# Asking for the up weights of the first pair of hidden tiles earlier in a macaron block

## The chip, the cores and the metric

The kernel runs on one core of one Trainium2 chip, in one launch. The metric is the device time of an execution in microseconds, as the median of several. Lower is better.

The core's engines work side by side, each through its own list of instructions: TensorE (PE in the profile; its weight loads are PEld), VectorE (DVE), ScalarE (ACT), GpSimd (POOL) and SyncE (SP), which issues most of the loads from DRAM. They wait for one another through semaphores.

## The reference

A macaron transformer block for 512 tokens of width 1024, in float32: a gated feed-forward network at half weight, a token mixer (differential and dilated attention), a second feed-forward network, and a last normalisation. The change lies in the two feed-forward networks, whose hidden width is 2816.

```python
def swiglu(x, w_gate, w_up, w_down):
    return (jax.nn.silu(x @ w_gate) * (x @ w_up)) @ w_down

x = x + 0.5 * swiglu(rmsnorm(x, ffn1_norm[layer]), ...)
x = x + token_mixer(rmsnorm(x, mix_norm[layer]), ...)
x = x + 0.5 * swiglu(rmsnorm(x, ffn2_norm[layer]), ...)
return rmsnorm(x, final_norm)
```

## The kernel before

**Layout and precision.** The activations lie transposed: eight tiles x[k] of 128 features by 512 tokens. Every factor of a product is split into a high part, rounded to fp32r, and a low part, the remainder; a product of two such factors is three matmuls (`mm3`, lines 108 to 111: high by high, high by low, low by high).

**A weight tile.** `get_w` (line 103) asks SyncE for 128 x 1024 values into a raw buffer (line 96; three buffers go round, `raw`), gives the tile a place in `w_all` (three places of 1024 high and 1024 low columns go round, `w_place`), rounds it on ACT (line 100) and makes the remainder on DVE (line 101). So a weight tile needs its raw buffer (until DVE has made the remainder of the tile three before it), its place (until PE has done with the tile three before it), the transfer, the cast and the remainder before PE can begin.

**A feed-forward network** (`ffn`, lines 184 to 512, called for "a", the first, and "b", the second) has JF = 22 hidden tiles of 128 and three stages:

- *Raw tiles*, j up to n1 - 1, where n1 (PAIRED) is 6 in "a" and 4 in "b": gate and up products side by side into banks pg and pu, each tile with two weight tiles of four features each (`wgu`, line 475), 48 matmuls of 512 columns. Below n0 (EARLY, 5 and 3) they use features that aren't yet normalised; the last, j = n0, uses the normalised ones, xh and xl. From j = n0 on the order of SyncE and POOL is that of the program text, PE's is so throughout, and on DVE and ACT a scheduler orders the raw tiles.
- *Pairs*, the tiles from n1 on, two by two, with a fast scheme for 2 x 2 blocks of a product: seven products of half size in place of eight, made of sums of weight blocks and of features. A unit is one pair and one side (gate or up). For the first pair only the gate side is such a unit; its up products are plain: `up(n1)` and `up(n1 + 1)` (line 272), 24 matmuls of 512 columns each, in banks of their own.
- *Down products*, eight output tiles of 66 matmuls each.

**Around the first pair.** `units[0]` is the gate side of the first pair, `units[1]` that of the second. What they need is made ahead:

- `weight_sums(j, c)` (line 261) makes two sums of weight blocks in two slots: SyncE loads one block (line 268) and POOL then adds another with an accumulating transfer (line 269). In the trace they are s10 and s30 for the gate side, s11 and s31 for the up side. Those of `units[0]` are asked for in the last raw tile, after k = 0 (line 488), those of `units[1]` as the pairs begin (line 429). In "a" the latter lie in slots 8 and 9, where the normalised features nx 0 and 1 lie until `normed_t(0)` has used them; in "b" they lie in slots 6 and 7.
- `normed_x(p)` makes the normalised features nx and splits them into xh and xl. `normed_t(p)` (line 235) makes their sums and splits them, into the tiles tx and tt of the trace (lines 241 to 257); it is called for p = 0 and 1 in the last raw tile, for p = 2 in `up(n1)` and for p = 3 in `up(n1 + 1)`.
- `load(0)` (line 296) asks for the two raw weight tiles of `units[0]`, raw_s0, in `up(n1)` after k = 2.
- In `up(n1 + 1)` `prepare_step` (line 415) begins to make the operands of the first products of `units[0]`: sums (`total`), casts (`high`, line 323) and remainders (`low`, line 327). They take their places from `w_all` too.

Within the pairs (line 492) DVE and ACT follow the program text as well. The up weights of the first pair, raw_su in the trace, are asked for and split at the start of each up product:

```python
            wh, wl = get_w(wst[j - n1][1], f"su{nm}{j}")
```

The first product of `units[0]` accumulates in a bank pw. With the trace's names the order on PE is: raw tiles on pg and pu, then `up(n1)` and `up(n1 + 1)` on pu, then pw, pz, px and so on.

Of the kernel before, what the change touches and what calls it, by code (L numbers as in the profile page):

```python
# [50 lines left out]
def tile_macaron(ctx: ExitStack, tc, xs, xT, wf, wgu1, wst1, wd1, wqk, wv, wo, wgu2, wst2, wd2,  # L51
# [13 lines left out]
    def slot(i, nm, dt=F32):  # L65
        return sl.tile([P, S], dt, tag=f"slot{i}", name=nm)

    def mm_bank(nm):
        return pp.tile([P, S], F32, tag="mm", name=nm, bufs=4)
# [24 lines left out]
    def load_w(src, nm, n=1024, shift=0):  # L94
        raw = wp.tile([P, 1024], F32, tag="raw", name=f"raw_{nm}")
        nc.sync.dma_start(raw[:, :n], src)
        return (raw, *w_place(shift))

    def split_w(raw, h, l, a, b):
        A.copy(h[:, a:b], raw[:, a:b])  # L100
        V.tensor_tensor(l[:, a:b], raw[:, a:b], h[:, a:b].bitcast(F32), op=ALU.subtract)  # L101

    def get_w(src, nm, n=1024, shift=0):
        raw, h, l = load_w(src, nm, n, shift)
        split_w(raw, h, l, 0, n)
        return h, l

    def mm3(po, wh, wl, mh, ml, first, last, on=False):
        T.matmul(po, wh, mh, start=first, stop=False, skip_group_check=on)  # L109
        T.matmul(po, wh, ml, start=False, stop=False, skip_group_check=on)  # L110
        T.matmul(po, wl, mh, start=False, stop=last, skip_group_check=on)  # L111
# [72 lines left out]
    def ffn(wgu, wst, wd, n0, n1, norm, early, res, nm, hooks, first=None, last_halves=None):  # L184
# [12 lines left out]
        def activated(j, t):  # L197
            h = ah[j] = slot(j, f"ah{nm}{j}", F32R)
            l = al[j] = slot(JF + j, f"al{nm}{j}", F32R)
            A.copy(h[:], t[:])  # L200
            V.tensor_tensor(l[:], t[:], h[:].bitcast(F32), op=ALU.subtract)

        def gate(j, pg, pu):
            t1 = tp.tile([P, S], F32, tag="ptb", name=f"t1{nm}{j}")
            if j < n0:
                bc = res["bc"]
                V.tensor_tensor(t1[:], pg[:], bc[:], op=ALU.mult)
                A.activation(t1[:], t1[:], AF.Silu)
                t2 = tp.tile([P, S], F32, tag="ob", name=f"t2{nm}{j}")
                V.tensor_tensor(t2[:], pu[:], bc[:], op=ALU.mult)  # L210
                V.tensor_tensor(t1[:], t2[:], t1[:], op=ALU.mult)
            else:
                A.activation(t1[:], pg[:], AF.Silu)
                V.tensor_tensor(t1[:], pu[:], t1[:], op=ALU.mult)
            activated(j, t1)
# [45 lines left out]
        def weight_sums(j, c):  # L261

            (a11, _), (a21, a22) = [[wst[j + i - n1][c][:, h * 512:(h + 1) * 512] for h in range(2)]
                                    for i in range(2)]
            sums[j, c] = []
            for i, (a, b) in enumerate(((a21, a22), (a11, a21))):
                t = slot(c * JF + j + i, f"s{2 * i + 1}{c}{nm}{j}")
                nc.sync.dma_start(t[:], a)
                nc.gpsimd.dma_start(t[:], b, accum_op=ALU.add)
                sums[j, c].append(t)  # L270

        def up(j):

            wh, wl = get_w(wst[j - n1][1], f"su{nm}{j}")
            pu = ups[j] = pp.tile([P, S], F32, tag="t", name=f"pu{nm}{j}", bufs=2)
            for k in range(KD):
                o = k // 2 * P + k % 2 * 4 * P
                o = slice(o, o + P)
                mm3(pu[:], wh[:, o], wl[:, o], xh[k][:], xl[k][:], k == 0, k == KD - 1)
                yield k  # L280

        ups = {}
        units = [(n1, 0)] + [(j, c) for j in range(n1 + 2, JF, 2) for c in range(2)]
        left, right = slice(0, HS), slice(HS, S)

        def pairs():
# [31 lines left out]
            def high(t):  # L318
                if not half:
                    h, l = w_place(ODD)  # L320
                    half.extend([(h[:, :512], l[:, :512]), (h[:, 512:], l[:, 512:])])
                made[t] = half.pop(0)
                A.copy(made[t][0], source(t))
# [91 lines left out]
            def prepare_step(t):  # L415
# [10 lines left out]
                if 0 <= t + 4 < steps:  # L426
                    high(t + 4)

            weight_sums(*units[1])
            for i in range(2):  # L430
                for k in up(n1 + i):
                    if i == 0 and k == 2:
                        load(0)
                    prepared(n1 + i, k)
                    if i == 1 and k % 2:
                        prepare_step(k // 2 - 4)
# [21 lines left out]
        def prepared(j, k):  # L458
            if (j, k) in prepare:
                f, p = prepare[j, k]  # L460
                f(p)

        order = ExitStack()
        for j in range(j0, n1):
            if j == n0:
                order.enter_context(tc.manual_schedule(engines={mybir.EngineType.SP,
                                                                mybir.EngineType.Pool}))
            mv = (eh, el) if j < n0 else (xh, xl)
            if j == 2 and first is not None:
                pg, pu = [pp.tile([P, S], F32, tag="t", name=f"p{c}{nm}2", bufs=2) for c in "gu"]  # L470
            else:
                pg = mm_bank(f"pg{nm}{j}")
                pu = mm_bank(f"pu{nm}{j}")
            for hf in range(2):
                wh, wl = get_w(wgu[j, hf], f"gu{nm}{j}_{hf}")
                for kk in range(4):
                    k = hf * 4 + kk
                    for c, pt in ((0, pg), (1, pu)):
                        o = kk * 256 + c * P
                        mm3(pt[:], wh[:, o:o + P], wl[:, o:o + P], mv[0][k][:], mv[1][k][:],  # L480
                            k == 0, k == KD - 1)
                    if (j, k) in hooks:
                        hooks[j, k]()
                        while due and "bc" in res:
                            gate(*due.pop(0))
                    prepared(j, k)
                    if (j, k) == (n0, 0):
                        weight_sums(*units[0])
            due.append((j, pg, pu))
            while due and "bc" in res:  # L490
                gate(*due.pop(0))
        with order, tc.manual_schedule(engines={mybir.EngineType.DVE, mybir.EngineType.Activation}):
            after_pairs(pairs())
        for m in range(KD):
# [8 lines left out]
            for c0 in range(0, JF, 8):  # L503
                n = min(8, JF - c0)
                wh, wl = get_w(wd[m, :, c0 * P:(c0 + n) * P], f"d{nm}{m}_{c0}", n * P)
                for kk in range(n):
                    k = c0 + kk
# [23 lines left out]
    with tc.manual_schedule(engines={mybir.EngineType.DVE, mybir.EngineType.Activation}):  # L531
        for t in range(4):
            raw = wp.tile([P, 1024], F32, tag="raw", name=f"raw_f{t}")
            h, l = w_place()
            for kk in range(2):
                k = 2 * t + kk
# [51 lines left out]
    n1 = {}  # L588
# [3 lines left out]
    for m in ffn(wgu1, wst1, wd1, EARLY[0], PAIRED[0], 0, early, n1, "a",  # L592
                 {(2, 2): spread, "down": bias_rows}, firsts):
        split_x(m, 1, xh[m], xl[m])
        square_x(m)
# [475 lines left out]
    for m in ffn(wgu2, wst2, wd2, EARLY[1], PAIRED[1], 2, early, n3, "b",  # L1071
                 {(0, 4): means, (0, 7): spread}, last_halves=last_halves):
        square_x(m)
# [90 lines left out]
```

## Time and profile before

| | us |
|---|---|
| median of 3 runs | 965.87 |
| lowest to highest | 965.36 to 966.94 |
| the profiled execution's own time | 965.61 |
| its span, from the first to the last instruction | 963.8 |
| PE busy (matmuls) | 947.6 |
| DVE busy | 595.6 |
| ACT busy | 477.2 |
| POOL busy | 87.5 |

Times within the trace count from the start of the span. A row of the timeline gives start, duration, engine, line of the kernel, operation, output and inputs, and in square brackets how long the engine stood idle before it and what released it. Matmuls overlap, so a matmul of 512 columns is shown with 0.39 us while the next begins earlier; the distance of starts is what counts. SPq is SyncE's queue, and a row there is the time in which a transfer is issued, not the transfer. A row of the waits gives total idle us, times and the longest. The mean TensorE clock granted was 0.996 of full speed.

### The profile page before, as it was taken

To read this page: it belongs to the slowest core of one execution; us is meant where nothing else is said; L and a number is where in the kernel's file an instruction comes from. 1 tells how busy PE (TensorE), PEld (TensorE's weight loads), DVE (VectorE), ACT (ScalarE), POOL (GpSimd) and SP (SyncE) were. 2 spreads that over 40 slices of the span, in tenths; PEclk is the share of its full clock that TensorE was granted. 3 is DMA by queue.
4 is the path that set the end of the run, shared out by engine and by line. 5 is a ranking of instruction groups with operands and counts; after the bars stand their busy time and mean duration, and the time that the engine had idled before them with its cause. 6 is when DMAs were issued, how large, how long until landed. Compare 5 with 4: busy or idle time off the path is not lost.

```text
span 963.8 us, 15503 instructions
## 1 busy us (share of the span) xinstructions
PE 947.6 (98%) x5934; PEld 852.8 (88%) x5934; DVE 595.6 (62%) x1173; ACT 477.2 (50%) x941; POOL 87.5 (9%) x98
## 2 busy tenths in 40 slices
PE   9999999999999999999999999999999999999996
PEld 7787999999788888988989888889999999988885
DVE  7697877777232336678764547697777787522223
ACT  7445665655222335566756645355656566422230
POOL 0011112110010110000000003210121210000110
PEclk9999999999999999999999999999999999999998
DMA  7157777864333351433333204545777774433312
GB/s 253 58 137 194 168 190 187 196 151 120 101 98 87 97 163 59 130 110 114 106 111 88 66 24 131 151 123 128 195 176 202 177 172 134 120 99 104 92 45 88
DMA packets 51162, 124.00 MB, mean 129 GB/s; under 512 B 5824, under 2 KB 8128, under 8 KB 51088
## 3 DMA queue, kind: packets, MB, share of 16 engines
q1 hardware_dynamic: 41696, 105.94, 35.3%
q0 software_dynamic: 9392, 17.08, 11.5%
q8 instruction: 46, 0.75, 0.3%
q14 instruction: 28, 0.23, 0.1%
HBM read 117.71 MB, written 2.14 MB: 124 GB/s over the span
## 4 chain that ended last, share of the span: by engine, by line
PE 90%; DVE 6%; ACT 2%; DMA 1%; issue 1%; SPq 0%; DVEq 0%; ACTq 0%
PE pda L109 4%; PE pda L110 4%; PE pda L111 4%; PE pdb L110 4%; PE pdb L109 4%; PE pdb L111 4%; PE po L833 2%; PE pwo L109 1%; PE pwo L110 1%; PE pwo L111 1%; PE pq L109 1%; PE pq L111 1%; PE pv L693 1%; PE pv L691 1%; PE pv L692 1%; PE pq L110 1%
## 5 line engine op out<-in xcount | busy, mean ns | idle before, releaser
L136 POOL TENSOR_TENSOR sq<-sq,sqt 128x512 f32<-128x512 f32 x20 | 28.0, 1398 | 464.7 <-ACT sqt L135 464.7
L109 PE MATMUL pda<-aha,w 128*128 128x512 f32 x176 | 68.6, 390 | 0.0
L110 PE MATMUL pda<-ala,w 128*128 128x512 f32 x176 | 68.5, 389 | 0.0
L111 PE MATMUL pda<-aha,w 128*128 128x512 f32 x176 | 68.5, 389 | 0.0
L101 DVE TENSOR_TENSOR w<-raw_db,w 128x1024 fp32r<-128x1024 f32 (+1 forms) x24 | 27.3, 1136 | 62.5 <-ACT w L100 62.5
L100 ACT CAST w<-raw_db 128x1024 fp32r<-128x1024 f32 (+1 forms) x24 | 23.5, 979 | 81.1 <-PE pdb L110 73.8
L101 DVE TENSOR_TENSOR w<-raw_da,w 128x1024 fp32r<-128x1024 f32 (+1 forms) x24 | 27.3, 1135 | 58.2 <-ACT w L100 58.2
L100 ACT CAST w<-raw_da 128x1024 fp32r<-128x1024 f32 (+1 forms) x24 | 23.5, 979 | 79.0 <-PE pda L110 55.2
L110 PE MATMUL pdb<-alb,w 128*128 128x512 f32 x154 | 59.9, 389 | 0.0
L109 PE MATMUL pdb<-ahb,w 128*128 128x512 f32 x154 | 59.9, 389 | 0.0
L111 PE MATMUL pdb<-ahb,w 128*128 128x512 f32 x154 | 59.9, 389 | 0.0
L799 DVE CUSTOM_DVE_ANT_0 pr<-sc,strip 128x128 f32<-128x128 f32 (+3 forms) x64 | 30.9, 489 | 33.3 <-PE sc L797 32.6
L802 ACT ACTIVATE pr<-pr,mx 128x128 f32<-128x128 f32 (+3 forms) x64 | 36.0, 563 | 30.9 <-DVE mx L799 29.9
L109 PEld LDWEIGHTS pda<-aha,w 128*128 128x128 f32 x176 | 33.0, 188 | 7.4 <-ACT w L100 0.5
L111 PEld LDWEIGHTS pda<-aha,w 128*128 128x128 f32 x176 | 33.0, 188 | 6.9
L110 PEld LDWEIGHTS pda<-ala,w 128*128 128x128 f32 x176 | 33.0, 188 | 6.8
L833 PEld LDWEIGHTS po<-v,ptb 128*128 128x128 f32 x240 | 32.7, 191 | 5.3 <-ACT ptb L823 2.7
L691 PE MATMUL pv<-w,xh 128*128 128x256 f32 x128 | 36.2, 283 | 0.0
L693 PE MATMUL pv<-w,xh 128*128 128x256 f32 x128 | 36.2, 283 | 0.0
L692 PE MATMUL pv<-w,xl 128*128 128x256 f32 x128 | 36.2, 282 | 0.0
L833 PE MATMUL po<-v,ptb 128*128 128x64 f32 (+1 forms) x240 | 32.5, 269 | 1.8 <-ACT ptb L823 1.7
L111 PEld LDWEIGHTS pdb<-ahb,w 128*128 128x128 f32 x154 | 28.9, 188 | 6.1
(528 smaller groups left out, 3329.7 us busy)
## 6 DMA issues: line engine op xcount, KB each, us to landing
raw_da<-wd_dram SPq DMA_DIRECT2D x16, 512.0 KB, 3.6
raw_qk<-wqk_dram SPq DMA_DIRECT2D x16, 512.0 KB, 3.7
raw_db<-wd_dram SPq DMA_DIRECT2D x16, 512.0 KB, 3.5
raw_s0b<-wst_dram SPq DMA_DIRECT2D x9, 512.0 KB, 4.7
raw_gua<-wgu_dram SPq DMA_DIRECT2D x8, 512.0 KB, 4.0
raw_s0a<-wst_dram SPq DMA_DIRECT2D x8, 512.0 KB, 4.8
raw_v<-wv_dram SPq DMA_DIRECT2D x8, 512.0 KB, 3.8
strip<-bias_rows SPq DMA_DIRECT2D x16, 256.0 KB, 3.8
```

The costliest lines, as they stand in the source:

```text
L100: A.copy(h[:, a:b], raw[:, a:b])
L101: V.tensor_tensor(l[:, a:b], raw[:, a:b], h[:, a:b].bitcast(F32), op=ALU.subtract)
L109: T.matmul(po, wh, mh, start=first, stop=False, skip_group_check=on)
L110: T.matmul(po, wh, ml, start=False, stop=False, skip_group_check=on)
L111: T.matmul(po, wl, mh, start=False, stop=last, skip_group_check=on)
L136: G.tensor_tensor(sq[:], sq[:], t[:], op=ALU.add)
L691: T.matmul(po, xh[k][:, xs], wh[:, o:o + 256], start=k == 0, stop=False)
L692: T.matmul(po, xl[k][:, xs], wh[:, o:o + 256], start=False, stop=False)
L693: T.matmul(po, xh[k][:, xs], wl[:, o:o + 256], start=False, stop=k == KD - 1)
L799: V.tensor_tensor_reduce(out=pi, in0=ps[:, :w], in1=st["b"][m][:, w - 1::-1], op0=ALU.add, op1=ALU.min, scale=1.0, scalar=3.0e38, accum_ou ...
L802: A.activation(pi, pi, AF.Exp, scale=-1.0, bias=st["mx"][:, m, i:i + 1], accum_out=st["ls"][:, m, i:i + 1])
L833: T.matmul(st["po3"][:, i, d0:d0 + dn], st["ptb", m, i][:, k * P:(k + 1) * P], vt[u // 4, k][:, fo + d0:fo + d0 + dn], start=k == 0, stop= ...
```

## The change

The request and split of the two up weight tiles of the first pair are taken out of `up` into a function of their own, `up_weights(j)`. The one for tile n1 is called in the last raw tile after k = 5, the one for tile n1 + 1 as the pairs begin, ahead of the sums of `units[1]` and of `up(n1)`. Both feed-forward networks run through this code. The rotation of the places in `w_all` stays as it was; in the rotation of the raw buffers tile n1 + 1's weights now come before the two raw tiles of `units[0]` and no longer after them.

```diff
         def up(j):
 
-            wh, wl = get_w(wst[j - n1][1], f"su{nm}{j}")
+            wh, wl = up_w[j]
             pu = ups[j] = pp.tile([P, S], F32, tag="t", name=f"pu{nm}{j}", bufs=2)
             for k in range(KD):
...
-        ups = {}
+        def up_weights(j):
+            up_w[j] = get_w(wst[j - n1][1], f"su{nm}{j}")
+
+        ups, up_w = {}, {}
         units = [(n1, 0)] + [(j, c) for j in range(n1 + 2, JF, 2) for c in range(2)]
...
+            up_weights(n1 + 1)
             weight_sums(*units[1])
             for i in range(2):
                 for k in up(n1 + i):
...
+                    if (j, k) == (n1 - 1, 5):
+                        up_weights(n1)
                     prepared(j, k)
                     if (j, k) == (n0, 0):
                         weight_sums(*units[0])
```

## The prediction

> **What bounds the kernel now.** I read the page first: its span, the busy shares and the chain that ended last.
>
> ```profile
> span 963.8 us, 15503 instructions
> PE 947.6 (98%) x5934; PEld 852.8 (88%) x5934; DVE 595.6 (62%) x1173; ACT 477.2 (50%) x941; POOL 87.5 (9%) x98
> PE 90%; DVE 6%; ACT 2%; DMA 1%; issue 1%; SPq 0%; DVEq 0%; ACTq 0%
> ```
>
> TensorE is busy for 98% of the span and carries 90% of the chain. The matmuls are the same before and after, in the same order, so a change of the time can only be TensorE's idle time that goes or comes. The list of waits of PE names idle time on the tile that the change concerns, pua (accumulator of an up product):
>
> ```profile
> PE pua L111 <- DVE w L101: 1.1, 2, 0.5
> PE pua L109 <- ACT w L100: 1.0, 2, 0.6
> ```
>
> Two waits for ACT's rounding of a weight tile and two for DVE's remainder of it. The busy times by stretch show where they lie, and what they cost. I put the bounds at starts of matmuls: the raw tile 5 of the first feed-forward block (62.77 to 73.65, the latter one interval after its last matmul), the two up products of tiles 6 and 7 (to 87.80), and the same two stages of the second block (639.67, 650.55, 661.44).
>
> ```profile
> 62.77:73.65 10.88, 10.88 (x49) 8.82 (x47) 7.24 (x15) 4.02 (x7) 1.72 (x2) 1.00 0.54 162
> 73.65:87.80 14.15, 12.05 (x49) 8.89 (x49) 11.55 (x22) 8.13 (x15) 1.75 (x2) 1.00 0.75 186
> 639.67:650.55 10.88, 10.88 (x49) 9.01 (x48) 10.47 (x21) 6.43 (x11) 1.25 (x2) 1.00 0.39 121
> 650.55:661.44 10.89, 10.89 (x49) 9.01 (x48) 8.61 (x18) 4.99 (x11) 0.49 (x1) 1.00 0.54 121
> ```
>
> Columns: stretch, its length, busy us and count of PE, PEld, DVE, ACT, POOL, then granted clock, DMA share, GB/s. All four hold 48 matmuls of 512 columns (the 49th lies across the bound). Three take 10.88 or 10.89 us, or 10.88 / 48 = 0.227 us each; the up stage of the first block takes 14.15. So the first block loses 14.15 - 10.88 = 3.27 us, and the second nothing. The clock is 1.00 in all four: none of the loss is clock. PE's timeline splits it:
>
> ```profile
> 73.42 0.39 PE L111 MATMUL pua<-xh,w 128*128 128x512 f32 x1
> 76.05 0.39 PE L109 MATMUL pua<-xh,w 128*128 128x512 f32 x1
> 80.61 0.39 PE L111 MATMUL pua<-xh,w 128*128 128x512 f32 x1
> 83.01 0.40 PE L109 MATMUL pua<-xh,w 128*128 128x512 f32 x1
> 87.80 0.28 PE L109 MATMUL pwa<-xh,w 128*128 128x256 f32 x1
> ```
>
> Four intervals lie between 73.42 and 76.05, where up(6) starts: 2.63 - 4 x 0.227 = 1.72 us lost. Between 80.61 and 83.01, where up(7) starts: 2.40 - 0.91 = 1.49. The remaining 0.06 are slightly long intervals behind them. Now the reason, from SyncE's queue and the two engines that split weights:
>
> ```profile
> 50.24 0.33 SPq L96 DMA_DIRECT2D raw_gua<-wgu_dram  x1
> 66.40 0.33 SPq L268 DMA_DIRECT2D s10a<-wst_dram  x1
> 66.96 0.33 SPq L268 DMA_DIRECT2D s30a<-wst_dram  x1
> 67.34 0.42 SPq L96 DMA_DIRECT2D raw_sua<-wst_dram  x1
> 67.80 0.90 SPq L301 DMA_DIRECT2D raw_s0a<-wst_dram  x2
> 75.69 0.33 SPq L96 DMA_DIRECT2D raw_sua<-wst_dram  x1
> 73.36 1.05 ACT L100 CAST w<-raw_sua 128x1024 fp32r<-128x1024 f32 x1 [3.92 <-DMA raw_sua<-wst_dram]
> 74.43 1.23 DVE L101 TENSOR_TENSOR w<-raw_sua,w 128x1024 fp32r<-128x1024 f32 x1 [4.27 <-ACT w L100]
> 75.58 0.42 DVE L241 TENSOR_TENSOR nxa<-nxa 128x256 f32<-128x256 f32 x1
> 80.30 1.05 ACT L100 CAST w<-raw_sua 128x1024 fp32r<-128x1024 f32 x1 [1.67 <-DMA raw_sua<-wst_dram]
> 81.38 1.23 DVE L101 TENSOR_TENSOR w<-raw_sua,w 128x1024 fp32r<-128x1024 f32 x1 [1.61 <-ACT w L100]
> ```
>
> The queue stands from 50.24 to 66.40 at s10a, the sums of unit 1, whose slots 8 and 9 still hold nx 0 and 1. Tile 6's up weights are queued behind them and asked for at 67.34, six us before PE wants them. Tile 7's are asked for at 75.69, the moment DVE has finished tile 6's split (74.43 + 1.23), because both use one of the three raw buffers. Each then pays transfer, 1.05 us of ACT and 1.23 us of DVE in a row while PE waits.
>
> **The change, part by part.** Nothing is added or removed; instructions move. In the changed order SyncE has: the last raw_gu tile, both raw_su tiles, s10 and s30, the two raw_s0 tiles. PE's and POOL's orders are the same. On ACT and DVE the two splits move up, in both blocks.
>
> *Tile 6, first block.* Its raw buffer is the one of the second half of raw tile 4, free when the 52.63 remainder ends; its place in w_all is that half's, whose matmuls end as raw tile 5 begins (62.77).
>
> ```profile
> 52.63 1.22 DVE L101 TENSOR_TENSOR w<-raw_gua,w 128x1024 fp32r<-128x1024 f32 x1
> 59.30 1.22 DVE L101 TENSOR_TENSOR w<-raw_gua,w 128x1024 fp32r<-128x1024 f32 x1
> 62.95 0.62 ACT L250 CAST txa<-nxa 128x512 fp32r<-128x512 f32 x1 [3.32 <-DVE nxa L242]
> raw_sua<-wst_dram SPq DMA_DIRECT2D x2, 512.0 KB, 5.3
> ```
>
> So the request goes out near 54 and has landed by 60 even at 5.3 us. Its cast stands behind the txa cast of 62.95: 63.6 to 64.6. Its remainder stands behind a Silu, the sum of gate tile 4 and two tta remainders: by my walk 66.9 to 68.1. PE wants it at 73.65: 5.5 us early. Gain 1.72.
>
> *Tile 7.* Its buffer is the one of raw tile 5's first half, free when the 59.30 remainder ends (60.52). Asked for at 60.5, landed at 65.8. Its place is that half's too, free after 24 matmuls: 62.77 + 24 x 0.227 = 68.2. On ACT it stands behind the third txa cast, which tile 6's remainder pushes to 69.1: cast 69.7 to 70.7, remainder 70.9 to 72.1. PE will want it at 73.65 + 24 x 0.227 = 79.1: 7 us early. Gain 1.49, and with the 0.06 the whole 3.27.
>
> *What is pushed back by this.* The first product of unit 0 would start at 87.80 - 3.27 = 84.53, and needs the remainder of its first operand, which DVE makes last:
>
> ```profile
> 86.19 0.68 DVE L327 TENSOR_TENSOR w<-raw_s0a,w 128x512 fp32r<-128x512 f32 x1
> 656.11 0.69 DVE L327 TENSOR_TENSOR w<-raw_s0b,w 128x512 fp32r<-128x512 f32 x1
> 661.44 0.28 PE L109 MATMUL pwb<-xh,w 128*128 128x256 f32 x1
> ```
>
> It ends now at 86.87, only 0.93 before 87.80. Does it come forward as well? DVE stood idle for 4.27 + 1.61 = 5.88 us in front of the two remainders, while the L241 subtraction behind the first, whose operands were ready long before, ran only at 75.58. DVE ran in program order; with both idle stretches gone the end is 86.87 - 5.88 = 81.0. My walk through the new orders gives 81.3 (Silu and product of tile 5 at 75.0 to 76.3, the four nx steps and four tta remainders of the last pair to 80.0, the sum to 80.6, then 0.68). The worst is that none of the idle goes: 86.87. I take 81.3, since both stretches were waits for transfers asked for early now; 3.2 us are spare, and the following remainders take 0.68 each against 1.42 us for a product (12 matmuls of 256 columns). If that cover went, each us beyond 84.53 would cost one. [...]
>
> *SyncE and POOL, first block.* s10 and s30 still wait for DVE's second tta remainder, about as late as now (66.4 to 67). The first raw_s0 request stays at about 67.4; the second now needs tile 6's remainder (68.1) instead of standing at 67.80 + 0.5. Its cover is PE until 84.53. Unit 1's requests come earlier, as they no longer need tile 7's split at 82.6. Cost nothing.
>
> *Second block.* PE lost nothing here, so nothing can be gained.
>
> ```profile
> 619.73 0.43 SPq L268 DMA_DIRECT2D s10b<-wst_dram  x1
> 636.11 3.00 SPq L301 DMA_DIRECT2D raw_s0b<-wst_dram  x2
> 642.68 1.14 ACT L250 CAST txb<-nxb 128x512 fp32r<-128x512 f32 x2
> 666.01 0.69 DVE L314 TENSOR_TENSOR s2b<-s10b,raw_s0b 128x512 f32<-128x512 f32 x1
> ```
>
> The sums of unit 1 move from 619.73 to behind tile 5's weights, which take the buffer that now goes at 636.11: some 17 us later, at 636.5. POOL's adds behind them follow, but the first reader is DVE at 666.01, 29 us on. Tile 5's cast waits for 24 matmuls from 639.67, to 645.1, and ends at 646.4; the second of the two txb casts of 642.68 stands behind it and slips from about 643.2, by 3.2 us. Were all of DVE's work behind to slip by that, the first remainder would end at 656.80 + 3.2 = 660.0, before 661.44. Cost between 0 and nothing measurable; I take 0.
>
> **Sum.** -1.72 - 1.49 - 0.06 + 0 = -3.27. The profiled execution took 965.61 (span 963.8 and 1.8 around it), 0.26 below the median of 965.87. 965.61 - 3.27 = 962.34 for an execution like it, 962.6 against the median. What follows is paced by PE, so it moves with it. A measurement here can tell about 0.2%, 1.9 us.
>
> **The rivals.** (a) Part of the gain stays behind: one tile's split is still late (962.6 + 1.49 or 1.72, about 964.2), or the wait moves to unit 0, the remainder ending at 86.87 against 84.53 and leaving 0.9 of gain (965.0). For it: 0.93 us of margin now, and a busier DMA stretch (0.75). Against: the walk. (b) The weights' request was not what PE waited for, and the time stays at 965.9. The rows against it: the two casts were released by the DMA of raw_sua. (c) Slower: tile 7's cast at ACT's head is held until up(6) has ended instead of up to 68.2, as it would be if its place in w_all were the one that up(6) still reads. It would start at 79.1 instead of 69.7, 9.4 us late; the txa casts, Silu of tile 5 and the first operand stand behind it; the remainder ends at 81.3 + 9.4 = 90.7 and unit 0 starts some 3 us later than at 87.80: 969. It turns slower once that cast starts after 69.7 + (87.6 - 81.3) = 76. Against: the places go round by three, and that of tile 7 is raw tile 5's first half.
>
> **How the numbers follow.** Forecast 0.82, (a) 0.10, (b) 0.02, (c) 0.06. The forecast's own range is 962.6 with 0.7 each way for the spread of the runs (965.36 to 966.94). The range reaches to the nearer case of (a): 961.9 to 964.3. Faster by over 0.2% (under 963.9): 0.82. Within: (a) and (b), 0.12. Slower: 0.06.
>
> **What would show it.** PE's waits for w on pua are gone, and the stretch from the first up matmul to the first pw matmul is 10.9 us in both blocks. SyncE asks for the two raw_su tiles ahead of s10, the second near 60.5; the casts of raw_sua lie near 63.6 and 69.7; the first L327 remainder ends near 81. A wait of PE on pwa in the first unit would prove the forecast wrong by (a) or (c), a longer wait on pub in the second block by the second-block step.

## The result and the profile after

The changed kernel takes 961.94 us (median of 6 runs, 961.72 to 963.22), against 966.09 for the kernel before (6 runs, 964.39 to 967.15). The ratio is 0.996, with a 95% interval of 0.9948 to 0.9973. The forecast was 962.6, from 961.9 to 964.3, so the median lies just above the lower end. Two later sets, on two chips, gave 0.9962 (0.9948 to 0.9975) and 0.9971 (0.996 to 0.9982); the medians fell by 4.15, 3.67 and 2.65 us in the three sets.

The page of the changed kernel, its span and busy times:

```profile
span 960.1 us, 15504 instructions
PE 946.5 (99%) x5934; PEld 853.1 (89%) x5934; DVE 595.6 (62%) x1173; ACT 476.5 (50%) x941; POOL 87.4 (9%) x98
```

The work is the same: DVE 595.6 us in both, ACT and POOL within 0.7. The span is 3.7 us shorter, and PE's share rose by one point: idle time went, as it had to.

PE's list of waits after the change, complete, behind two lines of the list before:

```profile
PE bcl L1041 <- DVE dgl L1037: 1.7, 1, 1.7
PE po L833 <- ACT ptb L823: 1.7, 1, 1.7
```

```profile
PE bcl L1047 <- DVE dgl L1043: 1.7, 1, 1.7
PE po L839 <- ACT ptb L829: 1.7, 1, 1.7
PE warm L528 <- POOL ones_d L522: 1.0, 1, 1.0
PE st_n L1031 <- ACT sql L1023: 0.9, 1, 0.9
PE sc L802 <- DVE mx L805: 0.6, 2, 0.4
PE pt L826 <- ACT ptb L829: 0.6, 1, 0.6
PE bc_n L178 <- DVE dg_n L174: 0.5, 1, 0.5
PE pga L109 <- ACT w L100: 0.2, 1, 0.2
```

The two lines on pua are gone and none has come; the lines in the attention and at the end (po, bcl) stand as before. The busy times by stretch, cut at the same matmuls as in the prediction:

```profile
62.72:73.60 10.88, 10.88 (x50) 9.01 (x48) 10.63 (x20) 5.81 (x9) 1.71 (x2) 1.00 0.56 180
73.60:84.48 10.88, 10.88 (x49) 9.01 (x48) 9.51 (x21) 6.12 (x13) 1.74 (x2) 1.00 0.67 150
636.31:647.19 10.88, 10.88 (x50) 9.01 (x48) 10.54 (x20) 5.88 (x10) 3.06 (x4) 1.00 0.86 241
647.19:658.08 10.89, 10.89 (x50) 9.01 (x48) 8.70 (x19) 5.54 (x12) 0.42 (x1) 1.00 0.40 76
```

The second row is the answer: 14.15 us have become 10.88, the 3.27 of the sum to the hundredth. Since 10.88 us is what 48 such matmuls take without a gap (0.227 us each), this says that both stalls are gone whole; the size, 3.27, is that of the stalls in the one traced execution of the kernel before. DVE's busy time shows where its work went: 7.24 and 11.55 us in the first two rows before, 10.63 and 9.51 now. The second network's rows have the lengths they had.

Of the 3.7 us between the two profiled spans, 0.05 lie ahead of 62.7 and 3.27 in this stretch; the first pw matmul of the second network moved from 661.44 to 658.08, by 3.36. The rest, some 0.35, lies at the very end.

The queue and the two splits (timelines of SyncE, ACT and DVE, kernel after):

```profile
50.18 0.33 SPq L96 DMA_DIRECT2D raw_gua<-wgu_dram  x1
53.85 6.99 SPq L96 DMA_DIRECT2D raw_sua<-wst_dram  x2
65.69 0.33 SPq L268 DMA_DIRECT2D s10a<-wst_dram  x1
66.90 0.33 SPq L268 DMA_DIRECT2D s30a<-wst_dram  x1
67.27 1.09 SPq L304 DMA_DIRECT2D raw_s0a<-wst_dram  x2
63.42 1.04 ACT L100 CAST w<-raw_sua 128x1024 fp32r<-128x1024 f32 x1
69.51 1.04 ACT L100 CAST w<-raw_sua 128x1024 fp32r<-128x1024 f32 x1
66.79 1.22 DVE L101 TENSOR_TENSOR w<-raw_sua,w 128x1024 fp32r<-128x1024 f32 x1
70.58 1.23 DVE L101 TENSOR_TENSOR w<-raw_sua,w 128x1024 fp32r<-128x1024 f32 x1
80.15 0.68 DVE L330 TENSOR_TENSOR w<-raw_s0a,w 128x512 fp32r<-128x512 f32 x1
84.48 0.28 PE L109 MATMUL pwa<-xh,w 128*128 128x256 f32 x1
```

A merged row of SyncE runs from its first issue to the end of its last, so the two raw_su requests went out at 53.85 and at 60.5 (53.85 + 6.99 less one issue of 0.33). The queue then stands at s10 as long as before, until 65.69, but nothing that PE needs stands behind. No row of ACT or DVE on raw_sua has an idle time in brackets any more. The last two rows are the margin: the first operand of unit 0 is ready at 80.83 and PE comes at 84.48.

### The profile page after: what moved, and what is told of

Same layout as the page of the kernel before. It is cut to its first block, busy times and chain, and to the rows that moved or that the text cites. A ratio compares the mean times of both kernels' runs of the same rounds, so it can differ in the third digit from the quotient of the medians.

```text
span 960.1 us, 15504 instructions
## 1 busy us (share of the span) xinstructions
PE 946.5 (99%) x5934; PEld 853.1 (89%) x5934; DVE 595.6 (62%) x1173; ACT 476.5 (50%) x941; POOL 87.4 (9%) x98
## 4 chain that ended last, share of the span: by engine, by line
PE 95%; DVE 3%; ACT 1%; issue 1%; DMA 0%; DVEq 0%; ACTq 0%
PE pda L109 4%; PE pda L110 4%; PE pda L111 4%; PE pdb L110 4%; PE pdb L109 4%; PE pdb L111 4%; PE po L839 2%; PE pua L109 1%; PE pua L111 1%; PE pua L110 1%; PE pwo L109 1%; PE pwo L110 1%; PE pwo L111 1%; PE pq L109 1%; PE pq L111 1%; PE pv L699 1%
```

## The experiments

All times are compared with runs of the kernel before on the same chip, in the same set.

**Which network.** The change itself, its half in the first network, its half in the second.

```diff
-            up_weights(n1 + 1)
+            if nm == "a":
+                up_weights(n1 + 1)
             weight_sums(*units[1])
...
-                    if (j, k) == (n1 - 1, 5):
+                    if nm == "a" and (j, k) == (n1 - 1, 5):
                         up_weights(n1)
```

(The edit is that of the first-only kernel, against the change; the second-only kernel has "b" in place of "a". In the other network each tile is asked for and split at the start of its up product, as before.)

> The change once more, beside kernels that hold one part of it. Theory (PE's two stalls in the first network were the whole loss): 3.3 us below before, the stretch from the first up matmul to the first pw matmul 10.9 us in both networks. Rival (the two earlier requests also help elsewhere, since the medians differed by 4.1 and not by 3.3): about 4 us below before, with a further stretch of some 0.8 us gone outside the first network's up stage.

> The early request and split in the first network only. Theory: all of the gain, 3.3 us below before and equal to the full change. Rival (the second network gains too, outside PE's listed waits): 0.4 to 0.8 us above the full change.

> The early request and split in the second network only. Theory: as before, within 0.5 us; the waits of PE on pua in the first network stand as they were, 2.1 us in total, and up to the first pw matmul of the second network nothing is gained. Rival: 0.4 to 0.8 us below before.

Measured: both 962.27, ratio 0.9962 (0.9948 to 0.9975); first only 962.04, 0.9959 (0.9945 to 0.9972); second only 966.19, 0.9996 (0.9987 to 1.0005). The first network has the whole gain, and the second none that shows. In the trace of the change of this set the stretch from the first up matmul to the first pw matmul is 10.89 us in the first network and 10.88 in the second. In the second-only kernel PE's list names pua again:

```profile
PE pua L109 <- ACT w L100: 0.8, 1, 0.8
PE pua L111 <- DVE w L101: 0.8, 2, 0.5
```

These are 1.6 us in place of the 2.1 that were expected: there tile 6's cast started at 72.5, not 73.36, so that its first matmul did not wait. The stretch, from 74.04 to 87.43, loses 2.51 us and not 3.27, although the program up to there is that of the kernel before. So the size of the stalls varies from execution to execution, and 3.27 is one value of it. The rival, a further gain outside, finds nothing in the second network.

**Which order.** Is it enough that SyncE's queue no longer stands at s10 when tile 6 is due? This is the kernel before with one call moved: request and split stay in the up product, and only the sums of unit 1 go behind the request of tile n1.

```diff
-            weight_sums(*units[1])
             for i in range(2):
                 for k in up(n1 + i):
+                    if i == 0 and k == 0:
+                        weight_sums(*units[1])
```

> Requests and splits of the up weights stay in the up products; only the sums of unit 1 are asked for behind those of tile n1, one call moved. Theory (SyncE's queue standing at s10 is the first cause, and the second tile is late only because it waits for the first's raw buffer): tile 6 asked for near 54 and its split done by about 71; tile 7 asked for near 71, landed by 77, cast before 79.1; both stalls gone, 3.3 us below before. Rival (each tile must have its own early request): only the stall of tile 6 goes, 1.7 us below before.

Measured: 963.58, ratio 0.9969 (0.9958 to 0.9981). Its SyncE and ACT:

```profile
54.27 0.33 SPq L96 DMA_DIRECT2D raw_sua<-wst_dram  x1
66.11 0.33 SPq L268 DMA_DIRECT2D s10a<-wst_dram  x1
70.66 0.33 SPq L96 DMA_DIRECT2D raw_sua<-wst_dram  x1
76.60 1.05 ACT L100 CAST w<-raw_sua 128x1024 fp32r<-128x1024 f32 x1 [3.00 <-DMA raw_sua<-wst_dram]
```

Tile 7 is still asked for only when tile 6's split frees the raw buffer they share, at 70.66, and its cast ends near 77.7; PE wants it near 79.5. PE waits nowhere on pua, and the stretch is 10.89 us (74.02 to 84.91), as in the change. So one moved call takes both stalls away; the second was a consequence of the first. The median lies 1.3 us above that of the change beside it; the up stage doesn't show where from, and the profiled execution has the half clock that is told of further on.

**Which tile.** Tile n1 early and tile n1 + 1 in its up product, and the other way round.

> Only tile n1's weights are asked for and split early; those of tile n1 + 1 stay in their up product, behind the two raw tiles of unit 0, in the raw buffer that tile n1's split frees. Theory (one chain): asked for near 68, landed by 74, cast ahead of 79; both stalls gone, 3.3 us below before. Rival (two separate causes, 1.72 and 1.49): 1.7 us below before, and PE still waits on pua where up(7) starts.

> Only tile n1 + 1's weights are asked for and split early; tile n1's stay behind the sums of unit 1. Theory: tile 6 is asked for at 67.3 as before, its cast starts near 73, and up(6) starts 1.3 to 1.7 us late as now; tile 7's stall of 1.49 is gone: 1.5 to 2 us below before. Rival (a transfer that has fewer raw tiles beside it lands in time for 73.65): both stalls gone, 3.3 us below before.

> Only tile n1 + 1's weights asked for and split early, with the places in w_all of the change for both tiles (in the run before this one the two places were exchanged, so that part of tile n1 + 1's products used other numbers). Theory: tile 6 asked for at 67.3, its cast starts near 73, up(6) loses 1.2 to 1.7 us; up(7) loses nothing; the stretch from the first up matmul's due time to the first pw matmul is 12.2 to 12.6 us, 1.5 to 2 us below before. Rival (two separate stalls of which an early landing removes the first too): 10.9 us, 3.3 us below before.

Tile n1 only: 962.83, ratio 0.9968 (0.9956 to 0.9981), no wait on pua, and a stretch of 10.89 us. Tile n1 + 1's weights are asked for at 69.01 and cast at 76.30 there. So the call of `up_weights(n1 + 1)` adds nothing to the gain; it adds spare time (a cast at 69.5 instead of 76.3).

Tile n1 + 1 only: 964.64, 0.9987 (0.9976 to 0.9999) with the places exchanged, and 964.86, 0.9985 (0.9976 to 0.9994) with the places of the change. In the profiled execution of the first of these, whose products of tile n1 + 1 use other numbers in part, up(6) starts on time, against the expectation, and only the wait for the remainder stands: the stretch is 11.91 us, a loss of 1.03. PE's timeline of the second:

```profile
72.86 0.39 PE L111 MATMUL pua<-xh,w 128*128 128x512 f32 x1
73.78 0.50 PE L109 MATMUL pua<-xh,w 128*128 128x512 f32 x1 [0.53 <-ACT w L100]
74.11 0.40 PE L110 MATMUL pua<-xl,w 128*128 128x512 f32 x1
75.03 0.50 PE L111 MATMUL pua<-xh,w 128*128 128x512 f32 x1 [0.52 <-DVE w L101]
...
85.62 0.28 PE L109 MATMUL pwa<-xh,w 128*128 128x256 f32 x1
```

up(6) is due at 73.09 (72.86 + 0.227), and the first pw matmul comes 12.53 us later, 1.65 more than 10.88: tile 6's stall (1.72 in the prediction) stands, tile 7's is gone. That is the expected split.

**A held cast, the condition of rival (c).** Tile n1 early; the call for tile n1 + 1 goes back into its up product, and the places are turned on, so that tile 7's cast must wait for up(6).

```diff
+            if j not in up_w:
+                w_used[0] += 2 if nm == "a" else 0
+                up_weights(j)
...
-            up_weights(n1 + 1)
             weight_sums(*units[1])
```

> Tile n1 early as in the change; tile n1 + 1's weights are split in their up product, and in the first network the place in w_all is turned on by two, so that they get the place that up(6) still reads: the condition of rival (c) of the prediction. Theory: the cast starts as up(6) ends, 79.1 to 79.5 instead of 69.5; up(7) starts 1.3 us late and loses 2.3 us in all; the first remainder of unit 0 ends 6.6 us behind the start of that cast, as it did before (80.30 and 86.87), near 86, when PE needs it near 86.8; so no further loss, 1.0 us below before. Rival, by the price in the prediction: everything behind the cast on ACT slips by 9.4 us, the first remainder ends near 90.7, and the time is 3 us above before.

Measured: 964.11, ratio 0.9984 (0.9975 to 0.9993). ACT, DVE and PE of this kernel:

```profile
74.34 0.62 ACT L200 CAST aha<-t1a 128x512 fp32r<-128x512 f32 x1 [0.82 <-DVE t1a L214]
78.80 1.04 ACT L100 CAST w<-raw_sua 128x1024 fp32r<-128x1024 f32 x1 [3.84 <-PE pua L110]
79.75 0.61 ACT L329 CAST w<-raw_s0a 128x512 fp32r<-128x512 f32 x1
79.88 1.23 DVE L101 TENSOR_TENSOR w<-raw_sua,w 128x1024 fp32r<-128x1024 f32 x1 [4.20 <-ACT w L100]
81.02 0.42 DVE L241 TENSOR_TENSOR nxa<-nxa 128x256 f32<-128x256 f32 x1
84.68 0.68 DVE L333 TENSOR_TENSOR w<-raw_s0a,w 128x512 fp32r<-128x512 f32 x1
86.28 0.28 PE L109 MATMUL pwa<-xh,w 128*128 128x256 f32 x1
```

ACT idles 3.84 us ahead of this cast, and the cast of raw_s0a behind it comes at 79.75 (75.17 in the change). DVE idles 4.20 us ahead of the remainder with the L241 subtraction behind, which comes at 81.02 (76.02 in the change). So both engines kept to their order in this trace. The first remainder of unit 0 ends at 85.36, 6.56 us behind the start of the cast, as in the kernel before (80.30 and 86.87). PE comes at 86.28 and doesn't wait for it. From the start of up(6), at 73.34, it is 12.94 us, a loss of 2.06 for tile 7's late split alone. In this order the held cast makes the kernel 2 us slower than the change and still faster than before.

It does not price rival (c) as the prediction has it. There the Silu of tile 5 and the casts of tx stand behind the held cast; here they stand ahead of it. An estimate for the prediction's order, from two traces: the held cast starts 5.46 us behind the start of up(6) (78.80 and 73.34), which is 79.06 in the change, in place of 69.51. In the change DVE is busy for 8.76 of the 9.02 us between the end of tile 7's remainder (71.81) and the end of the first remainder of unit 0 (80.83), so hardly any idle time could take up the delay: that end would come near 90.4, some 2.6 us behind 87.80, where unit 0 starts in the kernel before. No run shows this case.

**A wait further on.** From the first pw matmul of the first network to that of the second some profiled executions take 573.6 us and others 575.2. That led to the wait on po, 1.7 us in the lists of both kernels. The clock there, in four stretches of the second-only kernel (columns as in the prediction; the granted clock is the third from the right):

```profile
545.00:550.00 5.00, 5.00 (x33) 4.26 (x31) 3.60 (x6) 4.15 (x7) 0.00 (x0) 1.00 0.00 0
550.00:552.50 2.50, 0.80 (x6) 0.60 (x6) 1.05 (x2) 2.43 (x6) 0.00 (x0) 1.00 0.00 0
552.50:555.90 3.40, 3.40 (x14) 2.82 (x14) 1.96 (x4) 0.51 (x1) 0.00 (x0) 0.57 0.14 24
555.90:560.00 4.10, 4.10 (x24) 3.48 (x23) 1.54 (x9) 2.48 (x9) 0.00 (x0) 0.94 0.28 112
```

PE idles in the second stretch, and in the next 3.4 us the granted clock is 0.57 (0.50 between 553 and 555). A test on top of the change: in that step PE does its six pwo matmuls ahead of the value product that waits.

```diff
-                    put(tv + step * i + (1 if quick else m + 2), 1, values, m, i)
+                    put(tv + step * i + (1 if quick else m + 2),
+                        10 if (u, m, i) == (6, 1, NQ - 1) else 1, values, m, i)
...
-            put(e, 7, scale)
+            put(e, 10 if u == 6 else 7, scale)
```

> The change, and in the last step of attention unit 6 PE does the six pwo matmuls of that step ahead of the value product that waits for ptb, so that its 1.7 us of idle time there is filled. Theory (that idle time costs its length, and in some executions also a stretch of half TensorE clock behind it): 1.3 to 1.7 us below the change when the clock holds in both, the wait of PE on po gone from the list, and no stretch with a granted clock of 0.5 between 545 and 565. Rival (the scale step of unit 6 or the evacuation of unit 7 becomes late instead): as the change, within 0.5 us, with a new wait on ot or sc.

> The change, to be compared on one chip with the kernels beside it. Theory: 3.3 us below before, no wait of PE on pua.

Measured in one set: 960.16 (959.62 to 960.36), ratio to before 0.9939 (0.9927 to 0.9951), and for the change beside it 963.51 (961.4 to 963.81), 0.9971 (0.996 to 0.9982). This is faster than both kernels. Its wait and its clock:

```profile
PE po L839 <- ACT ptb L829: 0.3, 1, 0.3
550.00:553.00 3.00, 3.00 (x21) 2.66 (x20) 2.26 (x10) 1.29 (x6) 0.00 (x0) 1.00 0.18 30
```

The idle time fell from 1.7 to 0.3. From the first pw matmul of the first network to that of the second the profiled execution takes 572.05 us, against 573.60 in that of the change in the first set, whose clock held: 1.5 us less, as expected. Its runs lie within 0.74 us where those of the change beside it spread over 2.4. That the median gained 3.35 and not 1.5 fits with executions of the change in which the half clock came too (the profiled one of that set has it, span 961.6); which single runs had it isn't shown, since only one execution of each kernel is traced in a set.

## Why the prediction was right

*What bounds the kernel, and the size.* The mechanism is as forecast: PE's idle time on pua goes, nothing else on PE moves, and the stretch falls to the length without a gap (14.15 to 10.88). Against the medians the fall was 4.15, with an interval of the ratio that holds 3.27 (0.9966). The 0.9 between them isn't explained by any step of the change: the traced spans differ by 3.7, and the half clock behind the wait on po, about 1.6 us, comes in some executions and not in others. That the median still fell into the range, 0.04 us above its lower end, is partly luck: the prediction had no term for this spread and none for the stalls' own, 2.51 us in another execution.

*Tile 6 and tile 7.* The request was forecast near 54 and came at 53.85; casts at 63.6 and 69.7, measured 63.42 and 69.51; remainders ending at 68.1 and 72.1, measured 68.01 and 71.81. The prediction gave each stall a cause of its own and a gain of its own. That is true of the sizes, 1.65 left when only tile 7 is early, but not of the causes: with tile 6 early, tile 7's stall went by itself in two kernels. The forecast time doesn't hang on this, since the change makes both moves. The profile before had shown it (tile 7 was asked for at 75.69, when tile 6's remainder ended), and the prediction quoted it and still counted two moves.

*The cover of unit 0.* Forecast 81.3, measured 80.83; the spare time is 3.65 us. Ahead of that operand DVE works almost without a pause, 8.76 of 9.02 us, so its work sets that time. The walk took DVE's work in program order, and the traces show it so: the L241 subtraction ran behind the remainder that DVE idled for, for 4.27 us in the kernel before and for 4.20 us in the held kernel. The operand came 6.04 us earlier than before (86.87 and 80.83), where the two idle stretches had added up to 5.88.

*SyncE, POOL and the second network.* s10 and s30 came at 65.69 and 66.90 (66.40 and 66.96 before). In the second network the cast of tile 5 started at 641.77, as raw tile 3's first half ended, as the prediction had it. Its sums of unit 1 went from 619.73 to 633.11; counted from the first pw matmul, 3.36 us earlier now, that is 16.7 us later (forecast some 17). PE lost nothing by it, and the second-only kernel agrees, with a ratio of 0.9996 (0.9987 to 1.0005).

*The rivals.* (a) and (b) did not come. (c) did not come either, since the places go round as the prediction said. Its condition alone doesn't make the kernel slower than before: in the held kernel the first remainder came 6.56 us behind the start of the cast and PE didn't wait for it. By the estimate above, what counts is how much stands behind the held cast: with the Silu and the casts of tx behind it, as the prediction priced it, the estimate comes near its figures (90.7, 3 us), and no run tests it.

## What to carry to other kernels

In a queue that works in order, look for the request that stands at its head waiting for a buffer, and count what stands behind it and when it is wanted: here one request for something needed far later stood at the head for 16 us. The weights behind it could have been asked for at 53.85, when their buffer came free, and went at 67.34; moving one call was enough. Two stalls in a row on tiles of one name may be one: see whether the second request went out when the first tile's buffer came free, and fix the first before paying for both. Two stretches with the same work, one with the stall and one without, give the size of the gain better than the sum of the listed waits, which was 2.1 us against 3.27.

## What the runs showed of the hardware

- The waits of PE on pua cost more than their listed time. The four stalls of the kernel before look alike; the first two are these.

```profile
73.42 0.39 PE L111 MATMUL pua<-xh,w 128*128 128x512 f32 x1
74.45 0.50 PE L109 MATMUL pua<-xh,w 128*128 128x512 f32 x1 [0.64 <-ACT w L100]
74.79 0.40 PE L110 MATMUL pua<-xl,w 128*128 128x512 f32 x1
75.71 0.50 PE L111 MATMUL pua<-xh,w 128*128 128x512 f32 x1 [0.53 <-DVE w L101]
76.05 0.39 PE L109 MATMUL pua<-xh,w 128*128 128x512 f32 x1
```

  After each stall the next matmul began 0.33 to 0.34 us later and not 0.227, and the list counts from the end that is shown for the matmul before (73.42 + 0.39), not from when the next would have begun (73.42 + 0.227); so 2.1 us listed were 3.27 lost.
- A wait of 1.7 us on po (2.09 us between starts) was followed by a granted clock of half for some 3.4 us in 5 of the 11 profiled executions that have this wait, at about 1.6 us of time, and not in the other 6. In the second-only kernel PE idled 1.70 us on po, and the six pwo matmuls of 512 columns behind it, from 552.82 on, came 0.42 to 0.43 us apart (0.227 in the up stage), at a granted clock of 0.50 between 553 and 555. Behind the stalls on pua, listed with 0.26 to 0.95 us each, the fall was not seen. In four of the five executions that have such stalls (before, second only, tile n1 + 1 only with the places exchanged, held) the granted clock is 1.00 between 40 and 100 us; in the fifth (tile n1 + 1 only, with the places of the change) all matmuls of 512 columns between 60 and 90 us but the two that waited are shown with 0.39 or 0.40 us, as in the stretches with a granted clock of 1.00, and not with the 0.62 or 0.63 of the stretch at 0.50. Why it comes in some executions only isn't shown by these runs.
